# Two context products of a gate block in one PSUM bank, and a token product in another pool of banks

## The chip, the cores and the metric

One Trainium2 chip, one core. The metric is the device time of one execution in microseconds, as the median of several runs.

## The reference, cut to what matters

The kernel computes one layer of a hybrid backbone over 512 latent tokens with a prefix of 256 context tokens: a Fourier head group and a bidirectional gated linear recurrence side by side, an output projection, and then a product-key expert layer (PEER) whose tables make up most of the run. The change lies in the gates of the recurrence:

```
def rglru_scan(xc, w_a, b_a, w_x, b_x, lam, h0, reverse):
    ...
    r = jax.nn.sigmoid(jnp.einsum('blhi,hij->blhj', xh, w_a.astype(jnp.float32)).reshape(b_, L, C) + b_a.astype(jnp.float32))
    i = jax.nn.sigmoid(jnp.einsum('blhi,hij->blhj', xh, w_x.astype(jnp.float32)).reshape(b_, L, C) + b_x.astype(jnp.float32))
    log_a = -LRU_C * r * jax.nn.softplus(-lam.astype(jnp.float32))
    a = jnp.exp(log_a)
    inp = jnp.sqrt(-jnp.expm1(2.0 * log_a)) * (i * xf)
...
        for d, rev in ((0, False), (1, True)):
            hcd, fin = rglru_scan(uc, ..., h_zero, rev)
            hxd, _ = rglru_scan(ux, ..., fin, rev)
```

Each of the two directions has two gates, `r` and `i`, and each gate is needed for the 256 context tokens and for the 512 latent tokens.

## The kernel before

Features lie on the 128 partitions, tokens along the free axis; context (256 columns) and tokens (512 columns) stand side by side in tiles of 768 columns from a pool of 35 such buffers (`bt`, named `b` in the rows). The recurrence's 512 features are four blocks of 128, k = 0 to 3. Every product is taken in split precision: `mm3` issues three matmuls (high x high, high x low, low x high) that add up in one PSUM region, lines 132 to 134.

PSUM has eight banks of 512 fp32 columns. The program's function `pst` hands them out by tag: five banks `ps`, one `pm` (modulation sums), two `pa` (the products of the GeLU branch, `gate_branch`, and later work). Where a tag has no free bank, the matmul that would write waits until the old content has been read.

For a block k the stage does, in the order that the code has (an order written out by hand and kept on TensorE, ScalarE and VectorE by `in_order`): `u_block(k)`, the input projection, whose result ScalarE copies out (`pad`); `conv(k)` on VectorE; `y_split(k)`, the split into high and low; and `gates(k)`. `gates(k)` makes eight products, for two directions times two gates a context product (256 columns) and a token product (512 columns), and ScalarE applies the Sigmoid to each and so moves it into a 768-column tile. GpSimd then multiplies the second gate by the block's input. `decays` (Exp, Tanh on ScalarE, a square on GpSimd, a product on VectorE) and `scans` (Sqrt on ScalarE, the linear recurrences on VectorE) follow for blocks 0 and 1 together, between the gates of block 1 and those of block 2. ScalarE loads another table when it changes from one kind of function to another (ACT_TABLE_LOAD).

The stretch of code around it, in its order:

```
    u_block(3)
    gate_weights(1)
    gates(1)
    y_split(2)
    conv(3)
    mod_cols(1)
    gate_branch(0)
    ...
    decays([0, 1])
    gate_branch(1)
    gate_weights(3)
    scans([0, 1])
    mod_cols(2)
    gate_branch(2)
    gates(2)
    gates(3)
    mod_cols(3)
```

`mod_cols(w)` loads a piece of the modulation weights (`wm`, 1 MB) and multiplies the piece before it (line 232); after `gates(3)` the slots that it frees take the Fourier weights `wf`, and `f_mm` multiplies with them. The listing that follows shows the functions that the change touches and what calls them; the whole rest, from the Fourier stage to the expert layer, is not touched.

Of the kernel before, what the change touches and what calls it, by code (L numbers as in the profile page):

```python
# [14 lines left out]
AF = mybir.ActivationFunctionType  # L15
# [4 lines left out]
C = 256  # L20
# [31 lines left out]
def build(tc, xT, ctxT, c2t, vecs, wm, wu, wf, wg, wgate, wo, wq, keys, u, v, urow, vrow,  # L52
# [12 lines left out]
    def act(o, i, f, bias=None, scale=None, **kw):  # L65
        if bias is not None:
            kw["bias"] = bias
        if scale is not None:
            kw["scale"] = scale
        return S.activation(o, i, f, **kw)  # L70

    def after(ins, prev, why):
        if prev is not None:
            tc.add_manual_dep(ins, prev.name,
                              mybir.DependencyInfo(mybir.DependencyClass.NoSync,
                                                   mybir.DependencyReason.DATA), reason=why)
# [26 lines left out]
    def tact(*a, **kw):  # L103
        ins = act(*a, **kw).ins
        after(ins, last[0], "activation table order")
        last[0] = ins

    def pst(tag="ps", n=512, dt=F32):
        return psum.tile([P, n], dt, tag=tag, name="ps_" + tag, bufs={"ps": 5, "pm": 1, "pa": 2}[tag])
# [21 lines left out]
    def mm3(ps, a, b, start, stop):  # L131
        PE.matmul(ps, a[0], b[0], start=start, stop=False)  # L132
        PE.matmul(ps, a[0], b[1], start=False, stop=False)  # L133
        PE.matmul(ps, a[1], b[0], start=False, stop=stop)  # L134

    def cut(pair, sl):
        return pair[0][:, sl], pair[1][:, sl]

    vec = cpool.tile([P, NV], F32, name="vec")
# [25 lines left out]
    def bt(dt=F32, n=L):  # L165
        return bp.tile([P, n], dt, tag="b", name="b")
# [220 lines left out]
    def gates(k):  # L387
        w, h = k // 2, k % 2
        y, yp = ys[k]
        for dr in range(2):  # L390
            gt = []
            for g in range(2):
                o = ((dr * 2 + g) * 2 + h) * P
                a = cut(gp[w], slice(o, o + P))
                psc = pst()
                psx = pst()
                mm3(psc[:, :C], a, cut(yp, slice(0, C)), True, True)
                mm3(psx, a, cut(yp, slice(C, L)), True, True)
                r = bt()
                o = (V_BA if g == 0 else V_BX) + 4 * dr + k  # L400
                tact(r[:, :C], psc[:, :C], AF.Sigmoid, bias=vec[:, o:o + 1])
                tact(r[:, C:], psx, AF.Sigmoid, bias=vec[:, o:o + 1])
                gt.append(r)
            G.tensor_tensor(gt[1], gt[1], y, op=ALU.mult)
            rr[k, dr], xx[k, dr] = gt
# [75 lines left out]
    gate_weights(0)  # L481
    conv(1)
    gates(0)
    y_split(1)
    conv(2)
    mod_cols(0)
# [5 lines that stand above are left out]
# [9 lines left out]
# [5 lines that stand above are left out]
# [166 lines left out]
    for k in range(8):  # L672
        psk[k] = out_mm(k, wpo[k], Ys if k < 4 else mr)
        if k == 1:
# [5 lines left out]
            r = bt(F32, 512)  # L680
# [166 lines left out]
    for h in range(8):  # L847
# [5 lines left out]
        for p in range(2):  # L853
            wp = split_w(raw, p, G) if h else wpq[p]
            ps = pst()
# [41 lines left out]
    for dst, src in ((posT, lambda a: PH[:, a]), (r1T, lambda a: IH[:, a, 0]), (r2T, lambda a: IH[:, a, 1]),  # L897
                     (ghT, lambda a: GH[:, a]), (glT, lambda a: GL[:, a])):
        ps = pst()
# [41 lines left out]
    for b, n, e in ((0, P, eidx), (1, TB, qp.tile([TB, P], I32, name="eB", bufs=1))):  # L941
        ps = pst()
# [22 lines left out]
    for ch in range(NCH):  # L965
# [14 lines left out]
        for q in range(TC // 4):  # L980
            ps = pst()
            for t in range(4):
                o = ps[:, t * P:(t + 1) * P]
                k, r = 2 * q + t // 2, t % 2
# [338 lines left out]
```

## Time and profile before

| | |
|---|---|
| median of 3 runs (lowest, highest) | 1462.14 us (1456.86, 1463.33) |
| the profiled execution's own time | 1457.23 us |
| its span | 1455.5 us |
| mean granted TensorE clock over the span | 0.986 |

The span is the time from the first to the last instruction that the profiler saw; the execution's time holds it and some 1.7 us around it. The profiled execution lies near the lowest of the three runs. Times in rows are microseconds from the span's start. PE is TensorE, PEld its weight loads, DVE VectorE, ACT ScalarE, POOL GpSimd. In a row of a timeline the first number is the start, the second the time that one instruction (or x of them in a row) took, and the bracket the idle time of the engine ahead of it and what ended that. Matmuls follow each other faster than each takes, so they overlap in the rows.

### The profile page before, as it was taken

Reading aid. Unit: us, or ns where it says so; the run is one execution under the profiler, and the core shown is the slowest. Engines: PE = TensorE matmul, PEld = TensorE weight load, DVE = VectorE, ACT = ScalarE, POOL = GpSimd, SP = SyncE. Lnnn points to the kernel's source line nnn. Section 1 sums busy time; section 2 is a strip of 40 time slices with the busy share of each in tenths; the row PEclk is TensorE's granted clock in tenths of the full one; section 3 lists DMA queues with packets and bytes.
Section 4 is the critical chain, followed back from the end, with each engine's and each line's share of the span. In section 5 each row is a group of like instructions: output and inputs, shape, how many; then the busy total and the mean of one; then the engine's idle time right before and its main releaser. Section 6 shows DMA issues by size and latency. Waiting matters only on the chain. (4 is left out here: it accounts for less than half of the span.)

```text
span 1455.5 us, 22655 instructions
## 1 busy us (share of the span) xinstructions
PE 1386.5 (95%) x8577; PEld 1282.2 (88%) x8577; DVE 1234.6 (85%) x2185; ACT 614.5 (42%) x882; POOL 685.3 (47%) x462
## 2 busy tenths in 40 slices
PE   6998898999989999999999999999999999899995
PEld 2776766888969999999999999999999999899995
DVE  5677876599987999598998889999898989999973
ACT  4567634433434656434343432434333343243351
POOL 0044163666520000465666757675675766644412
PEclk9999999999999999999999999999999999999997
DMA  9334465331326999999999998999999999999901
GB/s 348 153 116 150 169 230 183 136 114 63 112 91 202 307 302 319 365 379 355 399 373 416 337 394 328 413 376 379 406 377 375 390 364 416 409 415 416 394 33 57
DMA packets 133645, 420.61 MB, mean 289 GB/s; under 512 B 10784, under 2 KB 60192, under 8 KB 110496
## 3 DMA queue, kind: packets, MB, share of 16 engines
q1 hardware_dynamic: 86976, 251.04, 46.5%
q0 software_dynamic: 46560, 168.14, 29.9%
q8 instruction: 67, 1.10, 0.3%
q14 instruction: 42, 0.34, 0.1%
HBM read 385.41 MB, written 33.69 MB: 288 GB/s over the span
## 5 line engine op out<-in xcount | busy, mean ns | idle before, releaser
L70 ACT ACTIVATE whi<-raw 128x1024 fp32r<-128x1024 f32 x296 | 312.7, 1060 | 589.1 <-PE ps_pa L133 291.6
L123 DVE TENSOR_TENSOR wlo<-raw,whi 128x1024 fp32r<-128x1024 f32 x264 | 327.0, 1241 | 41.4 <-ACT whi L70 39.3
L132 PE MATMUL ps_pa<-h2h,whi 128*128 128x352 f32 x1024 | 334.9, 327 | 3.2 <-ACT act L70 3.2
L134 PE MATMUL ps_pa<-h2h,wlo 128*128 128x352 f32 x1024 | 333.0, 325 | 0.2 <-DVE wlo L123 0.2
L133 PE MATMUL ps_pa<-h2l,whi 128*128 128x352 f32 x1024 | 332.6, 325 | 0.0
L1106 POOL DMA_INDIRECT row<-vrow,eidx x128 | 193.4, 1511 | 131.9 <-DVE oacc L1127 95.1
L1106 POOL DMA_INDIRECT row<-urow,eidx x128 | 198.3, 1549 | 110.7 <-DVE row L1113 56.8
L133 PE MATMUL ps_ps<-wl,whi 128*128 128x352 f32 x640 | 207.3, 324 | 0.0
L134 PE MATMUL ps_ps<-wh,wlo 128*128 128x352 f32 x640 | 206.7, 323 | 0.1
L132 PE MATMUL ps_ps<-wh,whi 128*128 128x352 f32 x640 | 206.1, 322 | 0.0
L132 PEld LDWEIGHTS ps_pa<-h2h,whi 128*128 128x128 f32 x1024 | 192.9, 188 | 5.3 <-ACT act L70 4.0
L134 PEld LDWEIGHTS ps_pa<-h2h,wlo 128*128 128x128 f32 x1024 | 192.7, 188 | 1.4 <-DVE wlo L123 0.5
L133 PEld LDWEIGHTS ps_pa<-h2l,whi 128*128 128x128 f32 x1024 | 192.7, 188 | 1.1
L1113 DVE SCALAR_TENSOR_TENSOR row<-row,hrow 128x1024 f32<-128x1024 f32 x128 | 153.6, 1218 | 32.6 <-DMA row<-urow,eidx 32.4
L1127 DVE SCALAR_TENSOR_TENSOR oacc<-row,gw,oacc 128x1024 f32<-128x1024 f32 x127 | 162.4, 1279 | 8.6 <-DMA row<-vrow,eidx 8.1
L134 PEld LDWEIGHTS ps_ps<-wh,wlo 128*128 128x128 f32 x640 | 120.2, 188 | 0.4 <-DVE wlo L123 0.4
L133 PEld LDWEIGHTS ps_ps<-wl,whi 128*128 128x128 f32 x640 | 120.2, 188 | 0.0
L132 PEld LDWEIGHTS ps_ps<-wh,whi 128*128 128x128 f32 x640 | 120.1, 188 | 0.0
L123 POOL TENSOR_TENSOR wlo<-raw,whi 128x1024 fp32r<-128x1024 f32 x32 | 77.5, 2422 | 84.1 <-ACT whi L70 57.8
L133 PE MATMUL ps_pa<-wl,whi 128*128 128x352 f32 x256 | 82.9, 324 | 0.0
L134 PE MATMUL ps_pa<-wh,wlo 128*128 128x352 f32 x256 | 82.6, 323 | 0.0
L132 PE MATMUL ps_pa<-wh,whi 128*128 128x352 f32 x256 | 82.3, 322 | 0.0
(303 smaller groups left out, 2606.4 us busy)
## 6 DMA issues: line engine op xcount, KB each, us to landing
raw<-u SPq DMA_DIRECT2D x64, 1024.0 KB
raw<-v SPq DMA_DIRECT2D x64, 1024.0 KB
Gd<-stg SPq DMA_DIRECT2D x22, 1024.0 KB
gt<-Gd SPq DMA_DIRECT2D x16, 1408.0 KB
raw<-wm SPq DMA_DIRECT2D x16, 1024.0 KB
b<-wm SPq DMA_DIRECT2D x32, 256.0 KB
raw<-wq SPq DMA_DIRECT2D x8, 1024.0 KB
Ad<-act SPq DMA_DIRECT2D x10, 704.0 KB
```

The source lines that it names most:

```text
L70: return S.activation(o, i, f, **kw)
L123: lo_ins[0] = (lo_eng or V).tensor_tensor(dst[1], src, dst[0].bitcast(F32), op=ALU.subtract).ins
L132: PE.matmul(ps, a[0], b[0], start=start, stop=False)
L133: PE.matmul(ps, a[0], b[1], start=False, stop=False)
L134: PE.matmul(ps, a[1], b[0], start=False, stop=stop)
L1106: G.indirect_dma_start(out=t, out_offset=None, in_=tab, in_offset=bass.IndirectOffsetOnAxis(ap=e[:, s:s + 1], axis=0))
L1113: ins = V.scalar_tensor_tensor(t, t, 1.0, hr, op0=ALU.mult, op1=ALU.mult, accum_out=dt[:, s:s + 1])
L1127: ins = V.scalar_tensor_tensor(o, t, g[:, s:s + 1], o, op0=ALU.mult, op1=ALU.add)
```

## The change

The two context products of a direction, 256 columns each, go to the two halves of one bank `both`, where each had a bank of its own. The token product of the second gate goes to a `pa` bank; that of the first gate stays in a `ps` bank. So a direction takes two `ps` banks and one `pa` bank where it took four `ps` banks. The instructions, their shapes and their order on each engine stay the same.

```
         for dr in range(2):
             gt = []
+            both = pst()
             for g in range(2):
                 o = ((dr * 2 + g) * 2 + h) * P
                 a = cut(gp[w], slice(o, o + P))
-                psc = pst()
-                psx = pst()
-                mm3(psc[:, :C], a, cut(yp, slice(0, C)), True, True)
+                psc = both[:, g * C:(g + 1) * C]
+                psx = pst("pa" if g else "ps")
+                mm3(psc, a, cut(yp, slice(0, C)), True, True)
                 mm3(psx, a, cut(yp, slice(C, L)), True, True)
                 r = bt()
                 o = (V_BA if g == 0 else V_BX) + 4 * dr + k
-                tact(r[:, :C], psc[:, :C], AF.Sigmoid, bias=vec[:, o:o + 1])
+                tact(r[:, :C], psc, AF.Sigmoid, bias=vec[:, o:o + 1])
                 tact(r[:, C:], psx, AF.Sigmoid, bias=vec[:, o:o + 1])
                 gt.append(r)
```

What each instruction waits for does change. TensorE's rows in `gates(0)`, first direction, before: the token product of the first gate, the context and token products of the second gate, and the first context product of the other direction (`ps_ps` and `ps_pa` are banks by tag with the tile's number, `b_515` and `b_516` the split input, `whi` and `wlo` the split gate weights):

```order
L132 MATMUL ps_ps_589<-b_515,whi_502 128x512
L133 MATMUL ps_ps_589<-b_516,whi_502 128x512
L134 MATMUL ps_ps_589<-b_515,wlo_503 128x512
L132 MATMUL ps_ps_599<-b_515,whi_502 128x256 [waits PE_49]
L133 MATMUL ps_ps_599<-b_516,whi_502 128x256
L134 MATMUL ps_ps_599<-b_515,wlo_503 128x256
L132 MATMUL ps_ps_600<-b_515,whi_502 128x512 [waits Activation_49]
L133 MATMUL ps_ps_600<-b_516,whi_502 128x512
L134 MATMUL ps_ps_600<-b_515,wlo_503 128x512
L132 MATMUL ps_ps_611<-b_515,whi_502 128x256 [waits Activation_49]
L133 MATMUL ps_ps_611<-b_516,whi_502 128x256
L134 MATMUL ps_ps_611<-b_515,wlo_503 128x256
```

The same place of the changed kernel (the bank of the first gate's context product is `ps_ps_588`):

```order
L132 MATMUL ps_ps_589<-b_515,whi_502 128x512
L133 MATMUL ps_ps_589<-b_516,whi_502 128x512
L134 MATMUL ps_ps_589<-b_515,wlo_503 128x512
L132 MATMUL ps_ps_588<-b_515,whi_502 128x256 [waits Activation_49]
L133 MATMUL ps_ps_588<-b_516,whi_502 128x256
L134 MATMUL ps_ps_588<-b_515,wlo_503 128x256
L132 MATMUL ps_pa_599<-b_515,whi_502 128x512
L133 MATMUL ps_pa_599<-b_516,whi_502 128x512
L134 MATMUL ps_pa_599<-b_515,wlo_503 128x512
L132 MATMUL ps_ps_610<-b_515,whi_502 128x256 [waits PE_49]
L133 MATMUL ps_ps_610<-b_516,whi_502 128x256
L134 MATMUL ps_ps_610<-b_515,wlo_503 128x256
```

No instruction has moved; the wait on ScalarE (Activation) now stands at the second gate's context product, and is gone from the token product and from the other direction's context product. The other seven (block, direction) pairs have the same wait at the same place.

ScalarE's rows at the end of `gates(3)` before: the last four Sigmoids, and the first split of the Fourier weights (`raw` to `whi`):

```order
L70 ACTIVATE b_989<-ps_ps_981,vec_72 128x256 [waits PE_49]
L70 ACTIVATE b_989<-ps_ps_982,vec_72 128x512 [waits PE_49]
L70 ACTIVATE b_1000<-ps_ps_992,vec_72 128x256 [waits PE_49]
L70 ACTIVATE b_1000<-ps_ps_993,vec_72 128x512 [waits PE_49]
L70 ACTIVATE whi_1018<-raw_1014 128x1024 [waits DMAHW2_49]
```

The same place of the changed kernel:

```order
L70 ACTIVATE b_982<-ps_ps_974,vec_72 128x256 [waits PE_49]
L70 ACTIVATE b_982<-ps_ps_975,vec_72 128x512 [waits PE_49]
L70 ACTIVATE b_992<-ps_ps_974,vec_72 128x256 [waits DVE_49,PE_49]
L70 ACTIVATE b_992<-ps_pa_985,vec_72 128x512 [waits PE_49]
L70 ACTIVATE whi_1010<-raw_1006 128x1024 [waits DMAHW2_49]
```

The last context Sigmoid has one wait more, on VectorE: its output tile (`b_992`, from the pool of 768-column buffers) stands in another buffer than `b_1000` did, which VectorE's last scan of blocks 0 and 1 reads.

## Rows read from the trace of the kernel before

**Rows 1.** page, busy time of TensorE, its share of the span and its instructions
```profile
PE 1386.5 (95%) x8577; PEld 1282.2 (88%) x8577; DVE 1234.6 (85%) x2185; ACT 614.5 (42%) x882; POOL 685.3 (47%) x462
```

**Rows 2.** busy time by stretch: TensorE, weight load, VectorE, ScalarE, GpSimd, clock, DMA
```profile
123.18:155.00 31.82, 31.73 (x155) 23.58 (x154) 23.24 (x21) 20.83 (x25) 11.40 (x6) 1.00 0.53 199
155.00:245.00 90.00, 79.59 (x424) 56.52 (x424) 64.37 (x80) 40.87 (x64) 43.88 (x26) 1.00 0.60 214
...
450.00:1400.00 950.00, 939.32 (x6236) 928.27 (x6235) 863.81 (x970) 384.08 (x524) 488.21 (x324) 0.99 0.97 367
```

**Rows 3.** TensorE's waits, 66 to 125 us: total, times, longest
```profile
PE ps_ps L132 <- ACT b L70: 7.9, 2, 7.3
```

**Rows 4.** TensorE in order of time, block 0's gates: start, duration
```profile
69.59 0.28 PE L132 MATMUL ps_ps<-b,whi 128*128 128x256 f32 x1
...
71.71 0.50 PE L132 MATMUL ps_ps<-b,whi 128*128 128x512 f32 x1 [0.57 <-ACT b L70]
...
73.57 0.28 PE L132 MATMUL ps_ps<-b,whi 128*128 128x256 f32 x1
```

**Rows 5.** ScalarE in order of time, block 0's gates
```profile
69.89 1.28 ACT L70 ACT_TABLE_LOAD   x1
71.19 1.06 ACT L70 ACTIVATE b<-ps_ps,vec 128x256 f32<-128x256 f32 x2
```

**Rows 6.** ScalarE's Sigmoids by shape, 68 to 124 us
```profile
L70 ACT ACTIVATE b<-ps_ps,vec 128x512 f32<-128x512 f32 x16 | 11.2, 702 | 1.3 <-PE ps_ps L134 1.3
L70 ACT ACTIVATE b<-ps_ps,vec 128x256 f32<-128x256 f32 x16 | 7.8, 484 | 0.2
```

**Rows 7.** TensorE in order of time, block 1's gates
```profile
83.01 0.28 PE L132 MATMUL ps_ps<-b,whi 128*128 128x256 f32 x1
...
83.37 0.40 PE L132 MATMUL ps_ps<-b,whi 128*128 128x512 f32 x1
...
84.06 0.28 PE L132 MATMUL ps_ps<-b,whi 128*128 128x256 f32 x1
...
86.25 1.06 PE L232 MATMUL ps_pm<-raw,cc 128*32 128x512 f32 x8
```

**Rows 8.** ScalarE in order of time, from block 1's gates to block 2's
```profile
83.66 3.87 ACT L70 ACTIVATE b<-ps_ps,vec 128x256 f32<-128x256 f32 x8
...
93.03 0.60 ACT L70 ACTIVATE gel<-ps_pa 128x512 f32<-128x512 f32 x1 [4.75 <-PE ps_pa L134]
...
114.34 3.33 ACT L70 ACTIVATE b<-ps_ps,vec 128x256 f32<-128x256 f32 x7
```

**Rows 9.** TensorE in order of time, gates of blocks 2 and 3
```profile
105.98 0.28 PE L132 MATMUL ps_ps<-b,whi 128*128 128x256 f32 x1
...
107.27 0.28 PE L134 MATMUL ps_ps<-b,wlo 128*128 128x256 f32 x1
114.87 0.80 PE L132 MATMUL ps_ps<-b,whi 128*128 128x512 f32 x1 [7.32 <-ACT b L70]
115.46 0.63 PE L133 MATMUL ps_ps<-b,whi 128*128 128x512 f32 x1
...
123.18 2.35 PE L232 MATMUL ps_pm<-raw,cc 128*32 128x512 f32 x20
```

**Rows 10.** ScalarE, TensorE and VectorE behind block 3's gates
```profile
129.14 1.06 ACT L70 ACTIVATE whi<-raw 128x1024 fp32r<-128x1024 f32 x1 [5.16 <-DMA raw<-wf]
...
131.48 0.40 PE L132 MATMUL ps_ps<-whi,b 128*128 128x512 f32 x1
...
125.61 2.67 DVE L433 TENSOR_TENSOR_SCAN b<-b 128x512 f32<-128x512 f32 x1
```

**Rows 11.** clock: TensorE by stretch (busy, granted clock, DMA), then in order of time
```profile
114.87:123.18 8.31, 8.31 (x34) 0.71 0.01 2
245.00:252.00 7.00, 6.64 (x25) 0.76 0.05 8
...
199.44 0.50 PE L132 MATMUL ps_ps<-b,whi 128*128 128x512 f32 x1 [2.33 <-DVE b L650]
```

More of the change, by code (lines that the diff above doesn't have):

```diff
@@ L391, in gates @@
             gt = []
+            both = pst()
             for g in range(2):
@@ L394, in gates @@
                 a = cut(gp[w], slice(o, o + P))
-                psc = pst()
-                psx = pst()
-                mm3(psc[:, :C], a, cut(yp, slice(0, C)), True, True)
+                psc = both[:, g * C:(g + 1) * C]
+                psx = pst("pa" if g else "ps")
+                mm3(psc, a, cut(yp, slice(0, C)), True, True)
                 mm3(psx, a, cut(yp, slice(C, L)), True, True)
@@ L400, in gates @@
                 o = (V_BA if g == 0 else V_BX) + 4 * dr + k
-                tact(r[:, :C], psc[:, :C], AF.Sigmoid, bias=vec[:, o:o + 1])
+                tact(r[:, :C], psc, AF.Sigmoid, bias=vec[:, o:o + 1])
                 tact(r[:, C:], psx, AF.Sigmoid, bias=vec[:, o:o + 1])
```

## The prediction

> **What bounds the kernel now.** I read the page first: TensorE is busy for 1386.5 of a span of 1455.5 us [rows 1]. Then the stretches: from 450 to 1400 us TensorE is at work for 939 of 950 us and the DMA engines for 97% of the time, while the change touches only the stage before that [rows 2]. So the question is how far the early stage ends sooner or later, and whether the rest moves with it. For the stage itself I read TensorE's waits between 66 and 125 us, where the four gate blocks stand. There are two on ScalarE, 7.9 us together, one of them 7.3 us [rows 3]; the rest of the stage is gapless. Both come from PSUM banks: five `ps` banks are full and the first Sigmoid has not yet read one of them. In block 0 TensorE issues five of its eight products and resumes at 71.71 us with the sixth [rows 4]; the Sigmoid that frees the bank starts at 71.19, right behind a table load [rows 5], and takes 0.48 us [rows 6]: 71.67, and 0.04 us to the matmul.
>
> **The change, part by part.** Eight (block, direction) pairs are touched. No instruction is added or removed and no matmul changes its shape. What changes is where the products go and what they wait for. The order listings show it: the second gate's context product, which waited for an old bank user, now goes into columns 256 to 511 of the bank that the first gate's context product has just filled, and waits for a ScalarE instruction; its token product goes to a `pa` bank and waits for nothing; the next direction's two products lose their waits on ScalarE. The ScalarE instruction awaited can only be the Sigmoid that reads columns 0 to 255, since the bank's earlier user was awaited by the product that opened it. So two banks' worth of room are won, but TensorE, which ran five products ahead of the first Sigmoid, may now run two ahead. The three that are lost are two context products and a token product.
>
> A context product (three matmuls) takes 0.36 us from start to start and a token product 0.69 us, read where nothing waits [rows 7]: 83.01 to 83.37 to 84.06. Three products are 0.36 + 0.69 + 0.36 = 1.41 us.
>
> *Block 0.* The release at 71.71 us comes from ScalarE's table load, which does not move. Before, three products were left, and the next work (the input projection of block 3) began at 73.57: 1.86 us [rows 4]. After, six are left: 3 x 1.05 = 3.15 us, 0.1 us more for the first matmul after a wait (0.50 us in [rows 4], 0.40 for its like in [rows 7]), and a second wait in the other direction. For that one I take the two bounds: nothing, if ScalarE has caught up; and the length of the two Sigmoids that ScalarE must do in between, 0.48 + 0.70 = 1.18 us [rows 6]. Following the chain (third Sigmoid when its product ends, fourth when the token product ends, fifth behind it) TensorE waits about 0.25 us and restarts with 0.1: 0.35 us. Sum 3.15 + 0.1 + 0.35 = 3.6, less 1.86: **+1.75 us**.
>
> *Block 1.* Before, no wait: the second gate's context product starts at 83.01 and the block's end is at 86.25, where the modulation matmuls begin [rows 7]. ScalarE starts its first Sigmoid of the block only at 83.66 [rows 8], since it copies out the input projection and splits weights first. It ends at 84.14, so the product waits 1.13 us and restarts with 0.1; the second direction costs 0.35: **+1.6 us**.
>
> *Do these 3.35 us reach the big wait, or are they lost in it?* They would be lost if the Sigmoid that ends it were set by something that does not move. It is not: ScalarE's chain to 114.34 us begins at 93.03 with the copy of the first branch projection, for which it had waited 4.75 us on TensorE [rows 8]. That copy moves with TensorE, and what follows up to 114.34 is ScalarE's own work and short waits for GpSimd and VectorE, which work on what it has just written.
>
> *Blocks 2 and 3.* TensorE has issued five products by 107.55 us (its last matmul starts at 107.27) and resumes at 114.87 [rows 9]. After the change it stops behind two, where it now starts the third product, 105.98, plus the shift. At the release three more products are left, 1.41 us at full clock. Block 2 then runs at the lower clock (below), where TensorE is slower than ScalarE and needs no further wait; block 3 has a wait in each direction, 0.35 us each: **+2.1 us**.
>
> *What moves behind it.* The modulation matmuls at 123.18 free the slot into which the next weights are loaded; ScalarE waits for that load until 129.14, and the Fourier product begins at 131.48 [rows 10]. TensorE has no gap from 123.18 to 155 us (31.73 of 31.82 busy) [rows 2]. So what is late at 123.18 is late at 155. I carry the shift to the end undiminished, since behind it follow stages with TensorE and DMA nearly full.
>
> *A wait that changes hands on ScalarE.* The second listing shows that the last context Sigmoid of block 3 now waits for VectorE as well: its output buffer is another one, read by the last scan of blocks 0 and 1. That scan ends at 125.61 + 2.67 = 128.28 [rows 10], 131.6 with the shift. Behind it stand one Sigmoid and the weight split that before began at 129.14. With the shift the weights land at 134.6; the two Sigmoids are done at 131.6 + 0.48 + 0.70 = 132.8. Hidden, with 1.8 us to spare; without the load as cover it would cost about 3 us.
>
> *The clock.* After the 7.3 us stop the granted clock averages 0.71 over the 8.31 us from the release [rows 11]: (1 - 0.71) x 2 x 8.31 = 4.8 us at 1.2 instead of 2.4 GHz. I take the same 4.8 us behind the longer stop, so it adds nothing. Bounds: the new stop in block 0 lasts 2.1 us (69.6 to 71.7). Behind a gap of 2.33 us at 199.44 the matmuls ran at full pace; behind one at 245 us, after a thin stretch, 7 us were granted 0.76 [rows 11], which is 3.4 us at the lower level and costs 1.7 us. So 0 to 1.7 us for each such place; I take 0, as the gap of 2.33 us is the nearer case.
>
> **Sum.** 1.75 + 1.6 + 2.1 = +5.5 us. The profiled execution took 1457.2 us, so its like would take 1462.7. The median shown, 1462.1, lies 4.9 us above it; against that the forecast is **1467.6 us**. About half a per cent, 7.3 us, is what a measurement of this kernel can tell from no change, so the likeliest verdict is no change, on the slow side.
>
> **A rule of the skill.** No row of the trace before shows one engine writing a bank while another reads it, since no bank there held two results with two readers. The Trainium skill's page "PSUM — Partial Sum Buffer", section "PSUM bank collisions raise a hardware error", says that a write by TensorE and a read by ScalarE in one bank must be kept apart by semaphores per bank, even for different columns. By that the wait in the listing is one that packing two readers into a bank brings along; without it the sum would be that of rival A.
>
> **Rivals.**
> A. *The run-ahead is gained, not lost* (the other side): if the second context product did not wait for the first Sigmoid, six banks would hold all of block 2, and TensorE would do eight products before the stop instead of five; three products fewer behind it. At full clock that is 0.69 + 0.36 + 0.69 = 1.7 us, at the lower clock twice that, 3.5; with block 0's 0.57 us, -2.3 to -4: 1458 to 1460. It decides whether the product is released by the first Sigmoid. The listing speaks against it. Chance 0.05.
> B. *The shift is swallowed later*: a load or VectorE chain between 155 and 245 us, where TensorE is idle for 10 of 90 us [rows 2], holds its old time, or the long stage at 97% DMA makes up for it. Then 1462 to 1465. Against: every wait I saw there hangs on a chain that TensorE itself started. Chance 0.12.
> C. *The clock drops once more*, in block 0, or stays low longer behind the 9 us stop: +1.7 to +3.4, 1469 to 1471. Chance 0.18.
> D. *ScalarE's new wait comes to bear*: if the last scan ends more than 1.8 us later than I put it, the weight split is late by the excess: +1 to +3, 1468.6 to 1470.6. Chance 0.07.
> The forecast itself, with a range of its own of 1465.5 to 1469.5 (the four second-direction waits between 0 and 0.7 us), has 0.58.
>
> **How the numbers follow.** Slower by over 0.5% means above 1469.4: most of C (0.15), half of D (0.04), and the forecast's upper edge (0.06): 0.25. Faster by over 0.5% needs more than A gives; 0.03 is for what the spread of the runs, 1456.9 to 1463.3, could do. No change: 0.72. The range 1460.5 to 1472 leaves out most of A and the tails of C.
>
> **What would show it.** In the profile after: TensorE's waits on ScalarE between 66 and 130 us grow from two to about eight, 7.9 us to about 13; the first stands before the second context product of block 0 and again ends at 71.7; block 1 has one of 1.1 us at 83.0 + 1.75; the long one grows from 7.3 to nearly 9 us; the modulation matmuls of 123.18 stand near 128.7, and the Fourier product of 131.48 near 137. Wrong: if the second context product starts before the first Sigmoid's end (A), if the shift is there at 137 but gone at 245 (B), if token matmuls of 0.63 us, as at 115.46 [rows 9], stand in block 0 or 1 (C), or if ScalarE's weight split starts later than the load's landing (D).

## The result and the profile after

The changed kernel took 1469.55 us (median of 6 runs, 1467.22 to 1473.46), the kernel before beside it 1462.55 us (6 runs, 1456.86 to 1463.33): a ratio of 1.0058, with a 95% interval of 1.0036 to 1.008. That is 7.0 us slower; the forecast was 5.5 us slower, 1467.6 us. The ratio lies just above the half per cent that was named as the bound to "no change", and its interval lies on both sides of that bound. The profiled execution has a span of 1467.2 us.

First the page's line of busy time, which answers to [rows 1], and TensorE's waits between 66 and 135 us (total, times, longest), which answer to [rows 3].

```profile
PE 1394.4 (95%) x8577; PEld 1287.5 (88%) x8577; DVE 1231.7 (84%) x2185; ACT 615.9 (42%) x882; POOL 688.1 (47%) x462
```
```profile
PE ps_ps L132 <- ACT b L70: 11.7, 3, 8.7
```

The instruction counts are those of before. TensorE waits for the same line of ScalarE, but 11.7 us instead of 7.9. Where those waits stand shows TensorE in order of time (start, duration, in brackets the idle time in front and who ended it):

```profile
69.64 0.39 PE L133 MATMUL ps_ps<-b,whi 128*128 128x256 f32 x1 [0.20 <-DVE b L123]
...
72.80 0.39 PE L132 MATMUL ps_ps<-b,whi 128*128 128x256 f32 x1 [1.97 <-ACT b L70]
...
73.56 0.63 PE L133 MATMUL ps_pa<-b,whi 128*128 128x512 f32 x1
...
77.59 0.28 PE L132 MATMUL ps_ps<-b,whi 128*128 128x256 f32 x1
...
88.21 0.39 PE L132 MATMUL ps_ps<-b,whi 128*128 128x256 f32 x1 [1.01 <-ACT b L70]
...
90.18 0.39 PE L134 MATMUL ps_ps<-b,wlo 128*128 128x512 f32 x1
90.67 0.39 PE L132 MATMUL ps_ps<-b,whi 128*128 128x256 f32 x1
90.90 0.28 PE L133 MATMUL ps_ps<-b,whi 128*128 128x256 f32 x1
...
91.93 1.06 PE L232 MATMUL ps_pm<-raw,cc 128*32 128x512 f32 x8
...
120.56 0.58 PE L132 MATMUL ps_ps<-b,whi 128*128 128x256 f32 x1 [8.73 <-ACT b L70]
...
126.43 0.39 PE L134 MATMUL ps_ps<-b,wlo 128*128 128x512 f32 x1
126.93 0.39 PE L132 MATMUL ps_ps<-b,whi 128*128 128x256 f32 x1
...
130.63 2.78 PE L232 MATMUL ps_pm<-raw,cc 128*32 128x512 f32 x24
...
138.92 0.40 PE L132 MATMUL ps_ps<-whi,b 128*128 128x512 f32 x1
...
206.85 0.79 PE L132 MATMUL ps_ps<-b,whi 128*128 128x512 f32 x1 [2.33 <-DVE b L651]
```

All three stops are now in front of a context product (256 columns) whose bank is named `ps`: the second gate's, behind two products. In [rows 4] and [rows 9] TensorE stopped in front of a token product (512 columns), behind five. The rows that answer to those of before: 73.57 has become 77.59, 86.25 has become 91.93 [rows 7], 123.18 has become 130.63 [rows 9], 131.48 has become 138.92 [rows 10], 199.44 has become 206.85 [rows 11]. So 7.45 us late at the modulation matmuls, 7.44 at the Fourier product, 7.41 at 199.44: what is lost by 131 us stays lost.

Not all of it is the change's. The second matmul of block 0's first gate product, which waits for the low part of the split input and stands ahead of all that the change delays, starts at 69.64 us. In the trace before it stands here:

```profile
68.56 0.39 PE L133 MATMUL ps_ps<-b,whi 128*128 128x256 f32 x1 [0.21 <-DVE b L123]
```

So this execution entered the stage 1.08 us late. Taking the difference of the same matmul's start in both traces, less that of the one in front, gives block 0: 77.59 - 73.57 - 1.08 = 2.94 us; block 1: 91.93 - 86.25 - 4.02 = 1.66; blocks 2 and 3: 130.63 - 123.18 - 5.68 = 1.77. The stage itself has lost 6.4 us.

ScalarE in order of time, and the stretches (length; busy time of TensorE, weight load, VectorE, ScalarE, GpSimd; granted clock; DMA):

```profile
70.97 1.28 ACT L70 ACT_TABLE_LOAD   x1
72.27 1.65 ACT L70 ACTIVATE b<-ps_ps,vec 128x256 f32<-128x256 f32 x3
...
132.47 0.47 ACT L70 ACTIVATE b<-ps_ps,vec 128x256 f32<-128x256 f32 x1 [2.45 <-DVE b L434]
132.84 0.68 ACT L70 ACTIVATE b<-ps_pa,vec 128x512 f32<-128x512 f32 x1
136.61 2.01 ACT L70 ACTIVATE whi<-raw 128x1024 fp32r<-128x1024 f32 x2 [3.09 <-DMA raw<-wf]
```
```profile
73.50:76.50 3.00, 3.00 (x10) 2.45 (x9) 2.67 (x5) 1.54 (x3) 1.07 (x1) 0.50 0.00 0
120.56:130.63 10.07, 9.87 (x42) 7.68 (x42) 9.93 (x7) 7.10 (x13) 6.98 (x3) 0.80 0.01 2
```

The first Sigmoid still starts right behind the table load (72.27), as in [rows 5], and TensorE goes on 0.5 us later, at 72.80; less the late entry that is 71.72, where the forecast had 71.7. The 2.45 us at 132.47 are ScalarE's new wait for VectorE; behind it stand the last two Sigmoids, and then ScalarE still waits 3.09 us for the weights. At 73.50 to 76.50 the granted clock is 0.50, 1.2 instead of 2.4 GHz, in a place where the trace before has none.

### The profile page after: what moved, and what is told of

Same layout as the page of the kernel before. It is cut to its first block, busy times and chain, and to the rows that moved or that the text cites. A ratio compares the mean times of both kernels' runs of the same rounds, so it can differ in the third digit from the quotient of the medians.

```text
span 1467.2 us, 22658 instructions
## 1 busy us (share of the span) xinstructions
PE 1394.4 (95%) x8577; PEld 1287.5 (88%) x8577; DVE 1231.7 (84%) x2185; ACT 615.9 (42%) x882; POOL 688.1 (47%) x462
```

## The experiments

**Pull the change's two halves apart.** The first gives each context product a bank of its own again and keeps only the move of the second token product to a `pa` bank. Against the kernel before:

```
-                psx = pst()
+                psx = pst("pa" if g else "ps")
```

> Each context product has a bank of its own again; only the second gate's token product stays in a pa bank. Theory 1 (the loss comes from the second context product, which shares its bank with the first and so waits for the first Sigmoid): no such wait is left and TensorE runs six products ahead of the first Sigmoid instead of two (five in the kernel before). Block 0 ends about 0.7 us earlier than before, block 1 as before, the wait in block 2 is shorter and one token product less stands behind it: about 1.5 us below the kernel before, 1461. Theory 2 (the loss comes from the pa bank, whose earlier reader stands late in ScalarE's order): as slow as the change, 1467 to 1470.

It took 1460.95 us (12 runs) against 1463.04, a ratio of 0.998 [0.9959, 1.0]. TensorE's waits between 66 and 135 us:

```profile
PE ps_ps L132 <- ACT b L70: 5.7, 1, 5.7
PE ps_pa L132 <- ACT gel L70: 0.7, 1, 0.7
```

One stop instead of three, of 5.7 us instead of 8.7, and a wait of 0.7 us for a `pa` bank. The stage comes out 0.8 us shorter than before, not longer: the move to the other pool does not make the loss.

The second keeps the shared bank and puts the second token product back into a `ps` bank:

```
-                psx = pst("pa" if g else "ps")
+                psx = pst()
```

> The two context products share a bank as in the change, but the second gate's token product stays in a ps bank. Theory 1: the second context product waits for the first Sigmoid at the same place, so the pa bank made no difference: within 1.5 us of the change, 5 to 7 us above the kernel before. Theory 2 (the pa bank is what costs): back near the kernel before, 1462 to 1464.

1469.58 us, a ratio of 1.0048 [1.0028, 1.0067], and the same three stops of 11.7 us, the longest 8.7. So the shared bank alone makes the loss.

**Sharing without the early reader.** The next kernel keeps both edits and changes the order of the instructions: both context products of a direction, then both token products, then the Sigmoids (`aw` holds the two gates' parts of the weights).

```
             both = pst()
+            for g in range(2):
+                mm3(both[:, g * C:(g + 1) * C], aw[g], cut(yp, slice(0, C)), True, True)
+            px = [pst("pa" if g else "ps") for g in range(2)]
+            for g in range(2):
+                mm3(px[g], aw[g], cut(yp, slice(C, L)), True, True)
             for g in range(2):
...
-                mm3(psc, a, cut(yp, slice(0, C)), True, True)
-                mm3(psx, a, cut(yp, slice(C, L)), True, True)
```

> The banks of the change, but both context products are issued ahead of both token products, and the four Sigmoids behind them. The bank is still shared, but no product waits for a Sigmoid of its own direction. Theory 1: all eight products of a block fit into four ps and two pa banks, so block 0 loses its wait of 0.6 us and ends 1.1 us earlier, and at the big stop of block 2 TensorE has all of block 2 and two products of block 3 behind it. The modulation matmuls of 123.18 come near 118.5. What comes next, the low part of the Fourier weights, stands on VectorE behind the scans that end at 129, 127.9 with the shift, so that the Fourier product starts only near 129 instead of 131.5: 2.5 us below the kernel before, 1460, with bounds of 1458.5 and 1461.5. Theory 2 (sharing a bank costs by itself, in whatever order): as slow as the change.

1462.11 us, 0.9994 [0.9975, 1.0014]: the loss is gone. TensorE now stops behind seven products of block 2 (eight were expected; the last waits for a `pa` bank that holds a product of `gate_branch`), for 3.41 us instead of 7.32. The stage's last modulation matmuls start at 120.29 us, 2.9 us sooner than in [rows 9], though this execution came in 1.7 us late. But the time is not better than before, and above the 1458.5 to 1461.5 us that were expected. TensorE shows why:

```profile
113.83 0.50 PE L132 MATMUL ps_pa<-b,whi 128*128 128x512 f32 x1 [3.41 <-ACT b L70]
...
120.29 2.78 PE L232 MATMUL ps_pm<-raw,cc 128*32 128x512 f32 x24
...
128.57 0.39 PE L132 MATMUL ps_ps<-whi,b 128*128 128x512 f32 x1
131.26 0.50 PE L133 MATMUL ps_ps<-wlo,b 128*128 128x512 f32 x1 [2.31 <-DVE wlo L123]
...
132.93 0.63 PE L133 MATMUL ps_ps<-wlo,b 128*128 128x512 f32 x1
```

The Fourier product starts at 128.57 and stops after one matmul, since VectorE has not made the low part of the weights; soon behind the stop matmuls run at 0.63 instead of 0.39 us. VectorE and GpSimd in order of time:

```profile
117.41 2.60 DVE L427 TENSOR_TENSOR b<-b 128x768 f32<-128x768 f32 x1
120.05 3.27 DVE L429 TENSOR_TENSOR_SCAN b<-b 128x768 f32<-128x768 f32 x1
123.24 2.53 DVE L427 TENSOR_TENSOR b<-b 128x768 f32<-128x768 f32 x1
125.81 2.22 DVE L432 TENSOR_TENSOR_SCAN b<-b 128x256 f32<-128x256 f32 x1
...
129.99 3.62 DVE L123 TENSOR_TENSOR wlo<-raw,whi 128x1024 fp32r<-128x1024 f32 x2
```
```profile
117.32 10.16 POOL L405 TENSOR_TENSOR b<-b 128x768 f32<-128x768 f32 x4 [9.24 <-PE ps_ps L134]
```

GpSimd's four products (second gate times input) now stand without a pause from 117.32 to 127.48, and four of VectorE's instructions in that time take 2.22 to 3.27 us.

**Take GpSimd out of it.** The same kernel, with the products of blocks 2 and 3 on VectorE:

```
-            G.tensor_tensor(gt[1], gt[1], y, op=ALU.mult)
+            (V if k > 1 else G).tensor_tensor(gt[1], gt[1], y, op=ALU.mult)
```

> As the run with both context products first, and in blocks 2 and 3 the product of the second gate with the block's input is done on VectorE, behind the scans, instead of on GpSimd, where it ran beside the scans from 117 to 127 us. Theory: what that run won at the stop (4.6 us by the branch product behind block 3) was given back because VectorE's scans, twice as long beside GpSimd's products, held up the low part of the Fourier weights. Without GpSimd beside them the scans take 6.3 us from 116.8 instead of 12.6, the four products 0.94 us each behind them, and the low part starts near 127.5, with the high part's end, instead of 130: the Fourier stage 2.5 to 3 us earlier than in that run, 1459.5. Rival: VectorE is held up by its own work, and the four products make it later: 1462 or above.

1460.01 us, 0.9989 [0.9962, 1.0017], span 1454.3. VectorE, then GpSimd, then TensorE:

```profile
115.39 0.95 DVE L427 TENSOR_TENSOR b<-b 128x768 f32<-128x768 f32 x1
116.38 1.76 DVE L429 TENSOR_TENSOR_SCAN b<-b 128x768 f32<-128x768 f32 x1
118.06 0.93 DVE L427 TENSOR_TENSOR b<-b 128x768 f32<-128x768 f32 x1
119.03 0.69 DVE L432 TENSOR_TENSOR_SCAN b<-b 128x256 f32<-128x256 f32 x1
119.75 1.28 DVE L434 TENSOR_TENSOR_SCAN b<-b 128x512 f32<-128x512 f32 x1
...
121.68 3.56 DVE L405 TENSOR_TENSOR b<-b 128x768 f32<-128x768 f32 x4
125.67 2.36 DVE L123 TENSOR_TENSOR wlo<-raw,whi 128x1024 fp32r<-128x1024 f32 x2 [0.43 <-ACT whi L70]
```
```profile
128.91 1.47 POOL L419 TENSOR_TENSOR b<-b 128x768 f32<-128x768 f32 x1 [22.85 <-ACT b L70]
```
```profile
126.99 0.39 PE L132 MATMUL ps_ps<-whi,b 128*128 128x512 f32 x1
```

The same four VectorE instructions take 0.95, 1.76, 0.93 and 0.69 us. The weights' low part starts at 125.67 instead of 129.99, though VectorE now also does the four products. Of these 4.3 us, 2.0 are an earlier entry into the stage than in the run with both context products first (68.26 against 70.28 us), so 2.3 us are left for the move. The Fourier product at 126.99 runs on, without the stop of 2.31 us; it was 131.48 before [rows 10]. Repeated unchanged, beside another set of runs of the kernel before:

> The version with both context products first and the gate product of blocks 2 and 3 on VectorE, once more, since its first interval reached from 0.9962 to 1.0017. By its trace the stage is 4.2 us shorter than in the kernel before, 0.29%: a ratio near 0.997 is expected, 1458 to 1459. If the rows' gain is taken back behind the stage, as it was without the move to VectorE, the ratio is 0.999 or more.

1459.78 us against 1463.83, 0.998 [0.9958, 1.0002], between the 0.997 that was expected and the rival's 0.999. Its Fourier product starts at 130.46, after entering the stage 1.3 us late: the stage is 2.3 us shorter than in the kernel before, not 4.2 as in the first of the two. The granted clock behind the stop differs, 0.61 over 8.77 us here and 0.75 over 6.91 us there; in contexts first, with 4.6 us, it was 1.00 over 6.46. At the gap that stood at 199.44 us [rows 11], counted from the entry, contexts first has kept 0.4 us of the 4.6 that it had won, and the two executions with the products on VectorE 4.2 of 4.2 and 1.6 of 2.3. Both medians are below the kernel before, neither clearly: a gain of 2 to 4 us, not settled.

**The terms one by one.** The whole change in blocks 0 and 1 alone, and in blocks 2 and 3 alone:

```
-            both = pst()
+            both = pst() if k < 2 else None
...
-                psc = both[:, g * C:(g + 1) * C]
-                psx = pst("pa" if g else "ps")
+                psc = both[:, g * C:(g + 1) * C] if both is not None else pst()[:, :C]
+                psx = pst("pa" if g and both is not None else "ps")
```

> The change in blocks 0 and 1 alone; blocks 2 and 3 have their four ps banks as before. Theory 1: the waits behind the first Sigmoid in blocks 0 and 1 are there (1.75 and 1.6 us, with a stretch at the lower clock in block 0 up to 2.9), and the big stop in block 2 hides none of it: counted from where the stage is entered, the shift is 3.35 us (to 4.6) at the release in block 2, and it stays the same to the Fourier product. 1466 to 1467. Rival: the delay of blocks 0 and 1 is swallowed by the big stop of block 2, and only blocks 2 and 3 cost: shift 0 behind the stop, the time that of the kernel before.

> The change in blocks 2 and 3 alone. Theory 1: no shift at the release in block 2, and 1.3 to 2.1 us at the modulation matmuls behind block 3; 1464.5 to 1465. Together with the run that has the change in blocks 0 and 1 alone it adds up to the shift of the whole change, 4.7 to 6.4 us in the stage. Rival: blocks 2 and 3 cost the whole of it, since the run-ahead is lost there: 4.7 to 6.4 us.

Blocks 0 and 1 alone: 1467.29 us against 1461.84, 1.004 [1.0023, 1.0057]. Blocks 2 and 3 alone (`k > 1`): 1465.53, 1.002 [1.0002, 1.0038]. TensorE where the long stop ends, first in blocks 0 and 1 alone, then in blocks 2 and 3 alone:

```profile
121.18 0.79 PE L132 MATMUL ps_ps<-b,whi 128*128 128x512 f32 x1 [7.32 <-ACT b L70]
```
```profile
115.64 0.58 PE L132 MATMUL ps_ps<-b,whi 128*128 128x256 f32 x1 [8.72 <-ACT b L70]
```

The long stop has its old length and its old place, a token product, where blocks 2 and 3 are as before, and the new ones where they are changed. Both times are a little above what was expected, and the medians, 5.5 and 3.7 us above the kernel before, add up to more than the 7.0 of the whole change; the intervals allow that.

**The scatter.** The changed kernel and the kernel before were each profiled once more:

> The changed kernel unaltered, once more, for a second profile. Theory 1: TensorE's waits stand at the same places again, second context products of blocks 0, 1 and 2, and the Fourier product starts 5.5 to 7.5 us later than before. If the stretch at the lower clock in block 0 belongs to the wait of 2 us there, it is in this profile too; if it depends on when the wait falls, it may be gone and block 0 costs 1.75 instead of 2.9 us. The shift that grew by some 4 us between 250 us and the end is expected to come out another way, since nothing in the change reaches there.

> The kernel before, unaltered, for a second profile. In the profile shown first no stretch at the lower clock lay in the first 100 us, while every later one of this study had one between 20 and 45 us, which costs 1 to 2.4 us ahead of the stage, and most grew by some 3 us more between 600 us and the end. If both are the clock's own and not the change's, this profile has a like shift against the first one, ahead of the gates and behind 600 us, and none between 68 and 131 us.

The changed kernel: 1469.91 us, 1.0052 [1.0031, 1.0073]. Its TensorE in block 0, and a stretch of it:

```profile
70.23 0.39 PE L133 MATMUL ps_ps<-b,whi 128*128 128x256 f32 x1 [0.20 <-DVE b L123]
...
73.40 0.38 PE L132 MATMUL ps_ps<-b,whi 128*128 128x256 f32 x1 [1.97 <-ACT b L70]
...
74.09 0.39 PE L133 MATMUL ps_pa<-b,whi 128*128 128x512 f32 x1
...
76.99 0.28 PE L132 MATMUL ps_ps<-b,whi 128*128 128x256 f32 x1
...
129.56 2.78 PE L232 MATMUL ps_pm<-raw,cc 128*32 128x512 f32 x24
...
205.77 0.50 PE L132 MATMUL ps_ps<-b,whi 128*128 128x512 f32 x1 [2.32 <-DVE b L651]
```
```profile
66.00:77.00 11.00, 8.74 (x47) 6.74 (x46) 8.45 (x15) 7.80 (x12) 1.48 (x1) 1.00 0.00 0
```

The stop in block 0 has the same 1.97 us, but the clock stays at 1.00 behind it, a token matmul takes 0.39 us and not 0.63, and the block loses 76.99 - 73.57 - 1.67 = 1.75 us, as the expectation had it for that case. The kernel before, run once more, took 1467.73 us with a span of 1466.0, 10.5 us more than its first profile, and its modulation matmuls stand here:

```profile
126.21 1.06 PE L232 MATMUL ps_pm<-raw,cc 128*32 128x512 f32 x8
```

That is 3.0 us behind [rows 9], with nothing changed: it entered the stage 2.2 us late and lost 0.8 in blocks 2 and 3, where nothing was expected. The late entry goes with a stretch at the lower clock between 40 and 50 us, which is absent only in the first profile of before and in the first one with the products on VectorE. From the gap at 199.44 us to the end the changed kernel took 4.3 and 3.5 us more than the first profile of before, much the same twice, against the expectation; but the kernel before took 7.5 us more there in its second profile, and the other seven profiles 1.2 to 4.8, with the new wait or without it. So an entry that is 1 to 2 us late, and differences of several us behind 200 us, belong to single executions and not to the change, and the first profile of before is the one that was quick. What the stage lost in each, worked out as above from the starts of the same matmuls (us against the first profile of before):

| kernel | late at entry | block 0 | block 1 | blocks 2, 3 | sum |
|---|---|---|---|---|---|
| forecast | | 1.75 | 1.6 | 2.1 | 5.5 |
| changed | 1.1 | 2.9 | 1.7 | 1.8 | 6.4 |
| changed, again | 1.7 | 1.8 | 1.6 | 1.3 | 4.7 |
| second token in `ps` | 2.4 | 1.8 | 1.6 | 1.4 | 4.8 |
| blocks 0, 1 alone | 1.7 | 2.9 | 1.6 | -0.5 | 4.1 |
| blocks 2, 3 alone | 0.8 | 0.0 | 0.0 | 2.1 | 2.2 |
| contexts apart | 1.8 | -0.7 | 0.0 | -0.1 | -0.8 |
| contexts first | 1.7 | -0.8 | 0.0 | -3.8 | -4.6 |
| first and VectorE products | -0.3 | -0.8 | 0.0 | -3.4 | -4.2 |
| first and VectorE products, again | 1.3 | -0.8 | 0.0 | -1.5 | -2.3 |
| before, again | 2.2 | 0.0 | 0.0 | 0.8 | 0.8 |

The two halves add up: 4.1 + 2.2 = 6.3, against 6.4 for both in the execution with the same clock in block 0. That they do so to 0.1 us is in part luck, since blocks 2 and 3 left as before came out at -0.5 in one profile and 0.8 in another.

## Why the prediction was right

**The mechanism.** It was as put: the second gate's context product waits for the Sigmoid that reads the other half of its bank, and TensorE runs two products ahead instead of five. With separate banks the loss is gone, with the token product back in `ps` it stays, and with both context products written before the first read it turns into a gain of the stage, 2.3 to 4.6 us. So it is not the sharing that costs but a write that stands behind a read of the same bank. The Trainium skill's page "PSUM — Partial Sum Buffer", section "PSUM bank collisions raise a hardware error", asks for a guard per bank even where the columns differ; the wait of 1.97 us in front of a product that writes other columns than the Sigmoid reads is such a guard, and the trace shows its price. No run here writes such a bank early without that wait.

**The terms.** Block 1 came out at 1.6 to 1.7 us (forecast 1.6), by a stop of 1.01 us (forecast 1.13) and a second one: from 90.18 to 90.67 is 0.49 us where 0.23 is usual, and the matmul behind it starts 0.1 late; together 0.37 us, forecast 0.35. Block 0 came out at 1.8 us (forecast 1.75) in two of the four profiles with the new wait there, and at 2.9 in the other two. Blocks 2 and 3 came out at 1.3 to 2.1 (forecast 2.1). Block 3's two waits are there, 0.35 us each as forecast (126.43 to 126.93 is 0.27 more than usual, and 0.1 for the restart). What scatters is the clock: the release is followed by 10.07 us at 0.80, which is (1 - 0.80) x 2 x 10.07 = 4.0 us at the lower level, against 4.8 in [rows 11], where the forecast carried over 4.8 as equal. Half of the 0.8 us is about what the blocks came out below the forecast, 1.8 instead of 2.1. Where the lower level does last 4.8 us, in blocks 2 and 3 alone, they cost 2.1:

```profile
115.64:126.10 10.46, 10.28 (x42) 8.08 (x42) 10.32 (x7) 7.18 (x13) 6.61 (x3) 0.77 0.01 2
```

In the changed kernel's second profile and with the second token in `ps` it lasts 3.1 and 2.9 us, and they cost 1.3 and 1.4.

**The clock.** "I take 0" for block 0 was the term that was mis-sized, where the profile of after is concerned. It is rival C, and it came in two of the four: 2.9 - 1.75 = 1.2 us, inside the bound of 0 to 1.7. The stop in front of it was equally long (1.96 or 1.97 us) with and without, so the row that the choice rested on, a gap of 2.33 us without a loss [rows 11], could not decide it; that gap itself is followed by a matmul of 0.79 us in the first profile of after, and of 0.50 in the second.

**The carry.** 7.45 us late at the modulation matmuls, 7.41 at the place of 199.44: rival B fell for that stretch. Rival A fell, since TensorE does two products ahead, not eight. Rival D's wait appeared, with 2.45 us, and was hidden as forecast: the two Sigmoids end at 132.84 + 0.68 = 133.52 (forecast 132.8), the weights are there at 136.61 (134.6).

**The sizes that were off.** "Two to about eight" waits: the view lists three, 11.7 us, and three of about 0.26 us, at 90.67, 126.93 and 129.39, are not listed; that makes six and 12.5 us, where about 13 us were forecast. And the whole: three comparisons with the new wait in all blocks give 1.0048 to 1.0058, 6.5 to 7.0 us in the medians and up to 8.5 by the ratio, while the stage lost 4.7 to 6.4. The intervals begin at 1.0028 to 1.0036, 4 to 5 us, so this can be the scatter of the long stage; from 199.44 us on the profiles with the new wait (1.6 to 4.8 us above the first of before) do not stand out from those without it (1.2 to 7.5), so no further loss there is shown. How much of the step over the bound is the clock in block 0 is open, since that is known of profiled executions alone; "no change" had 0.72 and "slower" 0.25, too sure for a forecast only 2 us below that bound.

**What an experiment's expectation missed.** For contexts first the next bound was named rightly, VectorE's low part of the weights, but put too early: GpSimd's products had come to stand beside VectorE's scans of blocks 0 and 1 without a pause. In the kernel before the first long scan had started 0.13 us ahead of GpSimd's next product (at 119.25) and took its own time:

```profile
119.12 1.76 DVE L428 TENSOR_TENSOR_SCAN b<-b 128x768 f32<-128x768 f32 x1
```

## What to carry to other kernels

Two results with different readers may share a PSUM bank if both are written before either is read; written, read, written again, the bank takes away TensorE's run-ahead, and the price is the products that it can no longer do during a stop that some other engine's chain sets. Write such pairs back to back, and then look for what the earlier TensorE makes start sooner: here GpSimd's products came to lie on VectorE's chain, and took most of the gain. Before you call a few microseconds a loss, subtract what the execution had already lost in front of the stage.

## What the hardware showed that was not expected

A VectorE instruction that starts while GpSimd's products stand in a row does not get slower by a share here: it takes its own time and about one GpSimd instruction more. Alone the four took 0.95, 1.76, 0.93 and 0.69 us, and a GpSimd product of 768 columns (line 419) 1.47 us; the sums with 1.47 are 2.42, 3.23, 2.40 and 2.16, measured were 2.60, 3.27, 2.53 and 2.22. The scan of 2.67 us in [rows 10] against 1.28 us alone is of the same kind. GpSimd is held up as well: 10.16 us for four, 2.54 each. The Trainium skill's page "SBUF — State Buffer", section "SBUF: two separate sides", says that a VectorE instruction with two inputs in SBUF and a GpSimd one that reads SBUF take a common pair of ports as an exclusive lock: the one that starts first has it for the whole instruction. By that rule the sums come out so, and the trace agrees to within 0.2 us; the scan that started first, at 119.12 us, was not held up.

And a stop of the same length, at the same instruction of the same kernel, was followed by a lower TensorE clock in one profiled execution (0.50 from 73.50 to 76.50 us) and not in the next (1.00 from 66 to 77 us).
